# Turning the SwiGLU products of two groups at once: transposes within partition quarters and an exchange through DRAM

## The chip, the cores and the metric

The kernel runs on one core of a Trainium2 chip. The metric is device time in microseconds (us) of one execution of the whole program. Engines are named as in the profile: PE (matmul), PEld (its weight load), DVE (VectorE), ACT (ScalarE), POOL (GpSimd), SP (SyncE, whose queue issues nearly all DMAs).

## The reference

One decoder layer in float32 on x of 256 tokens by 2048 features, DEPTH 1:

```python
x = layer_norm(ALPHA * x + 0.5 * swiglu_ffn(x, ffn1_...), ln1_g, ln1_b)
u = x @ w_in + b_in                     # q, k, v and the convolution's input
mixed = concat([attention(q, k, v, sinks), conformer_conv(conv_in)]) @ w_out + b_out
x = layer_norm(ALPHA * x + mixed, ln2_g, ln2_b)
x = layer_norm(ALPHA * x + 0.5 * swiglu_ffn(x, ffn2_...), ln3_g, ln3_b)

def swiglu_ffn(x, w_gate, w_up, w_down):
    h = silu(x @ w_gate) * (x @ w_up)   # 256 x 5632
    return h @ w_down
```

The two FFNs hold most of the work: three matrices of 2048 x 5632 each. The change is in them alone.

## The kernel before, in words

Every matrix operand is split into a high and a low part of the matmul's reduced float32 type: ACT casts the raw tile to `hi` (L133) and DVE subtracts it to get `lo` (L135). A product is then three matmuls, `hi*hi`, `hi*lo` and `lo*hi` (`mm3`, L466 to L468), added up in PSUM.

**Order of the work.** Each engine runs its instructions in the order in which the program writes them; waits are semaphores. The class `Steps` sets that order by hand. A step is one weight tile of 128 x 1024: its 12 matmuls for both token blocks of 128, then `st.step()`, which runs what is due by the table `later` (`st.at(delay, work, after)`), splits up to two weight tiles ahead, and then runs what is due with `after` set. Weights come by SP into `raw` (4 buffers), are split into `hi` and `lo` (8 buffers each, RING), and may run LEAD = 7 tiles ahead of PE. A `raw` buffer is loaded anew as soon as both its readers are through, so SP's weight load waits for DVE's `lo`.

**An FFN.** The 5632 hidden features are 44 chunks of 128. They are taken in parts, `(0, JA)` and `(JA, JT)` with JA = 24, so 24 and then 20 chunks. In a part, first groups of two chunks: eight steps give gate and up products for 256 features in PSUM, with tokens on the partitions (`token_group`). `group` then applies Silu on ACT (`sl`, L658) and multiplies on DVE (`ht`, L659). The down product contracts over the features and needs them on the partitions, so `turn` (L666) transposes: DVE's transpose works in blocks of 32 x 32, and one instruction covers 32 partitions and 128 columns, reading one quarter of the partitions (t) and writing another (f). That is 16 instructions for a group, four in each of steps 1 to 4 after the group; in step 5 ACT casts the result to `hh` (L670) and DVE forms `hl` (L671). When the part's groups are done, `tokens_by` runs the down products: for each of four blocks c of 512 output columns, half as many steps as the part has chunks; at a block's end DVE adds the PSUM sum to `xt` (`evacuate`, L299). `psB` and `psC` have two PSUM buffers each, used in turn by the groups' products and the column blocks' sums.

Between the FFNs stand the mixer (attention and convolution) and the layer norms. `prepare3` loads the last layer norm's rows and has ACT load its square root table. It is called after the last group of FFN2 and before its last down products.

## Time and profile before

| | us |
|---|---|
| runs | 1716.37 median of 3 (1715.96 to 1716.41) |
| the profiled execution, span from first to last instruction | 1713.9 |
| PE busy | 1702.6 |
| PEld busy | 1416.3 |
| DVE busy, of it transposes L666 | 1183.7, 212.8 |
| ACT busy | 808.7 |
| POOL busy | 206.2 |
| down products of FFN1 begin | 266.16 (first part) |

The profiled execution's own time is its span of 1713.9 us; the runs' times are 2.5 us longer, for what lies around the span. Busy times of the engines overlap. A line of the profile that names groups reads: line of the kernel, engine, operation, output<-inputs, shapes, count, then busy time and mean ns of one, then idle time of the engine before them with what ended it. A line of a timeline gives the start, the duration and the same names. A line on DMAs gives KB each and the median time from issue to landing. A line on waits gives who waited for whom, total, times and the longest.

### The profile page before, as it was taken

To read this page: it belongs to the slowest core of one execution; us is meant where nothing else is said; L and a number is where in the kernel's file an instruction comes from. 1 tells how busy PE (TensorE), PEld (TensorE's weight loads), DVE (VectorE), ACT (ScalarE), POOL (GpSimd) and SP (SyncE) were. 2 spreads that over 40 slices of the span, in tenths; PEclk is the share of its full clock that TensorE was granted. 3 is DMA by queue.
4 is the path that set the end of the run, shared out by engine and by line. 5 is a ranking of instruction groups with operands and counts; after the bars stand their busy time and mean duration, and the time that the engine had idled before them with its cause. 6 is when DMAs were issued, how large, how long until landed. Compare 5 with 4: busy or idle time off the path is not lost.

```text
span 1713.9 us, 21604 instructions
## 1 busy us (share of the span) xinstructions
PE 1702.6 (99%) x7857; PEld 1416.3 (83%) x7857; DVE 1183.7 (69%) x2021; ACT 808.7 (47%) x1044; POOL 206.2 (12%) x116
## 2 busy tenths in 40 slices
PE   9999999999999999999999999999999999999997
PEld 7888888888888888888888888888888888888886
DVE  7877776545777765658888788877764467777655
ACT  6544444334444443477665465444443344444431
POOL 0000000000000000168996200000000000000000
PEclk9999999999999999999999999999999999999999
DMA  9766655666656656555754557655556656665662
GB/s 317 259 205 194 195 191 192 196 196 190 193 195 195 191 191 196 170 176 190 203 178 159 196 187 244 209 196 192 192 189 201 194 190 195 196 193 191 233 206 75
DMA packets 96299, 336.38 MB, mean 196 GB/s; under 512 B 11200, under 2 KB 11328, under 8 KB 95936
## 3 DMA queue, kind: packets, MB, share of 16 engines
q1 hardware_dynamic: 96048, 334.74, 60.7%
q8 instruction: 61, 1.00, 0.2%
q14 instruction: 46, 0.38, 0.1%
q10 hardware_dynamic: 144, 0.26, 0.0%
HBM read 332.86 MB, written 2.10 MB: 195 GB/s over the span
## 4 chain that ended last, share of the span: by engine, by line
PE 99%; DVE 0%; DMA 0%; ACT 0%; issue 0%; DVEq 0%; SPq 0%
PE grp L468 18%; PE grp L467 18%; PE grp L466 18%; PE acc L466 11%; PE acc L467 11%; PE acc L468 11%; PE in_c L789 2%; PE in_a L789 2%; PE in_q L789 1%; PE in_a L787 1%; PE in_c L787 1%; PE grp L487 1%; PE grp L488 1%; PE grp L485 1%; PE in_q L787 1%; PE tp L339 0%
## 5 line engine op out<-in xcount | busy, mean ns | idle before, releaser
L133 ACT CAST hi<-raw 128x1024 fp32r<-128x1024 f32 (+1 forms) x616 | 643.0, 1047 | 762.7 <-PE grp L468 357.9
L135 DVE TENSOR_TENSOR lo<-raw,hi 128x1024 fp32r<-128x1024 f32 (+1 forms) x543 | 660.4, 1221 | 386.2 <-ACT hi L133 382.1
L466 PE MATMUL grp<-hi,xcat 128*128 128x512 f32 x1384 | 538.4, 389 | 0.0
L467 PE MATMUL grp<-lo,xcat 128*128 128x512 f32 x1384 | 538.4, 389 | 0.0
L468 PE MATMUL grp<-hi,xcat 128*128 128x512 f32 x1384 | 538.4, 389 | 0.0
L467 PEld LDWEIGHTS grp<-lo,xcat 128*128 128x128 f32 x1384 | 259.8, 188 | 54.1
L466 PEld LDWEIGHTS grp<-hi,xcat 128*128 128x128 f32 x1384 | 259.8, 188 | 53.9
L468 PEld LDWEIGHTS grp<-hi,xcat 128*128 128x128 f32 x1384 | 259.8, 188 | 53.8
L466 PE MATMUL acc<-hi,hh 128*128 128x512 f32 x708 | 274.7, 388 | 0.0
L468 PE MATMUL acc<-hi,hl 128*128 128x512 f32 x708 | 274.6, 388 | 0.0
L467 PE MATMUL acc<-lo,hh 128*128 128x512 f32 x708 | 274.6, 388 | 0.0
L135 POOL TENSOR_TENSOR lo<-raw,hi 128x1024 fp32r<-128x1024 f32 x73 | 175.9, 2432 | 730.3 <-ACT hi L133 723.4
L666 DVE STREAM_TRANSPOSE hf<-ht 32x128 f32<-32x128 f32 x704 | 212.8, 302 | 11.2
L466 PEld LDWEIGHTS acc<-hi,hh 128*128 128x128 f32 x708 | 132.9, 188 | 27.3
L467 PEld LDWEIGHTS acc<-lo,hh 128*128 128x128 f32 x708 | 132.9, 188 | 27.2
L468 PEld LDWEIGHTS acc<-hi,hl 128*128 128x128 f32 x708 | 132.9, 188 | 27.2
L852 DVE SCALAR_TENSOR_TENSOR conv<-hc,cw_sb,conv 128x256 f32<-128x256 f32 x231 | 96.7, 485 | 1.1
L449 POOL TENSOR_SCALAR rs_t<-rs_y,rs_w 128x1 f32<-128x1 f32 x1 | 0.3, 342 | 717.9 <-DVE rs_y L448 717.9
L299 DVE SCALAR_TENSOR_TENSOR xt<-acc,xt 128x512 f32<-128x512 f32 x46 | 31.7, 690 | 54.7 <-PE acc L468 54.7
L658 ACT ACTIVATE sl<-grp 128x256 f32<-128x256 f32 x88 | 33.6, 384 | 56.5 <-PE grp L468 52.7
L466 PE MATMUL acc<-hi,mh 128*128 128x512 f32 x128 | 50.5, 394 | 0.0
L659 DVE TENSOR_TENSOR ht<-sl,grp 128x256 f32<-128x256 f32 x88 | 36.5, 418 | 20.3 <-ACT sl L658 20.2
(149 smaller groups left out, 947.6 us busy)
## 6 DMA issues: line engine op xcount, KB each, us to landing
raw<-in_wu SPq DMA_DIRECT2D x348, 512.0 KB, 4.3
raw<-in_wd SPq DMA_DIRECT2D x176, 512.0 KB, 4.3
raw<-in_win SPq DMA_DIRECT2D x52, 512.0 KB, 4.0
raw<-in_wout SPq DMA_DIRECT2D x32, 512.0 KB, 4.0
xt<-in_xT SPq DMA_DIRECT2D x8, 256.0 KB, 5.8
raw<-in_head SPq DMA_DIRECT2D x8, 256.0 KB, 4.7
xt<-in_x SPq DMA_DIRECT2D x2, 1024.0 KB, 8.0
rg<-in_rows SPq DMA_DIRECT2D x8, 256.0 KB, 4.4
```

The source lines that it names most:

```text
L133: nc.scalar.copy(hi, raw)
L135: eng.tensor_tensor(out=lo, in0=raw, in1=hi.bitcast(F32), op=ALU.subtract)
L299: nc.vector.scalar_tensor_tensor(out=y, in0=ps, scalar=factor, in1=x_, op0=ALU.mult, op1=ALU.add)
L466: nc.tensor.matmul(ps, s_hi, m_hi, start=start, stop=False)
L467: nc.tensor.matmul(ps, s_hi, m_lo, start=False, stop=False)
L468: nc.tensor.matmul(ps, s_lo, m_hi, start=False, stop=stop)
L658: nc.scalar.activation(sl, ps[b][:, : JG * P], AF.Silu)
L659: nc.vector.tensor_tensor(out=ht[:, b], in0=sl, in1=ps[b][:, JG * P :], op=ALU.mult)
L666: nc.vector.transpose(dst[:, t], src[:, f])
L787: nc.tensor.matmul(ps[:, :S], w[1][:, n], x1[:, k, 0, :], start=False, stop=k == KT - 1)
L789: nc.tensor.matmul(ps, w[0][:, n], x1[:, k], start=k == 0, stop=False)
L852: nc.vector.scalar_tensor_tensor(out=out, in0=x_, scalar=w, in1=acc, op0=ALU.mult, op1=ALU.add)
```

## The change

- Three parts instead of two in each FFN: 12, 16 and 16 chunks (`PARTS`).
- Two groups share one tile `ht`. After every second group one transpose of 128 x 1024 turns all 32 x 32 blocks in place, each within its own quarter of the partitions (`hr`). Four DMAs then write the quarters of `hr` to a buffer in DRAM (`far`), each in runs of 1 KB, one step later; a fifth DMA reads the buffer back as `hf` with the quarters exchanged, another step later. The cast to `hh` and the subtraction for `hl` follow two steps after that, on 1024 columns at once. `ht`, `hr` and `hf` take turns in two buffers of one tag.
- The features now lie on the partitions in another order inside four chunks; the rows of the down weights are put in the same order when the inputs are laid out (`turned`), and `block` picks the 128 x 128 block that a matmul takes.
- `down_order`: in the part of 12 chunks the first two column blocks run their first four steps each before their last two. The parts of 16 run in plain order.
- `prepare` of the last part is called 6 steps into the down products, and the rows `g3` live in another tag.

```diff
-JA = 24
+PARTS = ((0, 12), (12, 28), (28, 44))
...
+    def down_order(n):
+        half, held = n // 2, 2 if n == 12 else 0
+        order = [(c, t) for c in range(2) for t in range(half - held)]
+        order += [(c, t) for c in range(2) for t in range(half - held, half)]
+        if held == 0:
+            order.sort()
+        return order + [(c, t) for c in range(2, NC_) for t in range(half)]
...
-                def group(j, ps, hh=hh, hl=hl):
-                    ht = pool.tile([P, 2, JG * P], F32, tag="ht", name="ht")
-                    hf = pool.tile([P, JG, S], F32, tag="hf", name="hf")
+                def group(g, ps, hh=hh, hl=hl, gated=gated):
+                    if g % 2 == 0:
+                        gated[:] = [pool.tile([P, 4, 2, P], F32, tag="ht", name="ht")]
+                    f = slice(2 * (g % 2), 2 * (g % 2) + 2)
                     for b in range(2):
                         sl = pool.tile([P, JG * P], F32, tag="sl", name="sl")
                         nc.scalar.activation(sl, ps[b][:, : JG * P], AF.Silu)
-                        nc.vector.tensor_tensor(out=ht[:, b], in0=sl, in1=ps[b][:, JG * P :], op=ALU.mult)
-                    def turn(f):
+                        sides = (x_.rearrange("p (f n) -> p f n", f=2) for x_ in (sl, ps[b][:, JG * P :]))
+                        nc.vector.tensor_tensor(out=gated[0][:, f, b], in0=next(sides), in1=next(sides), op=ALU.mult)
+                    if g % 2:
+                        st.at(1, lambda ht=gated[0]: turn(g // 2, ht), True)
+
+                def turn(g, ht):
+                    hr = pool.tile([P, 4, 2 * P], F32, tag="ht", name="hr")
+                    nc.vector.transpose(hr.rearrange("p f n -> p (f n)"), ht.rearrange("p f b n -> p (f b n)"))
+                    st.vector(1.2)
+                    far = dram.tile([4, 32, 4, 2 * P], F32, tag="far", name="far")
+                    def write():
                         for t in range(4):
-                            src = ht[32 * t : 32 * t + 32].rearrange("p b (j f n) -> p f b j n", j=JG, n=32)
-                            dst = hf[32 * f : 32 * f + 32].rearrange("p j (b t n) -> p t b j n", b=2, n=32)
-                            nc.vector.transpose(dst[:, t], src[:, f])
-                    for f in range(4):
-                        st.at(1 + f, lambda f=f: turn(f), True)
-                    st.at(5, split, True)
+                            nc.sync.dma_start(far[:, :, t].rearrange("f r n -> r f n"), hr[32 * t : 32 * t + 32])
+                    def read():
+                        hf = pool.tile([P, 8 * P], F32, tag="ht", name="hf")
+                        nc.sync.dma_start(hf, far.rearrange("f r t n -> (f r) (t n)"))
+                        st.at(2, lambda: split(hf), True)
+                    def split(hf):
+                        full = hf.rearrange("p (t k i) -> p k t i", t=4, k=8)
+                        hi, lo = (x_[:, g].rearrange("p b j (t i) -> p (b j) t i", t=4) for x_ in (hh, hl))
+                        nc.scalar.copy(hi, full)
+                        nc.vector.tensor_tensor(out=lo, in0=full, in1=hi.bitcast(F32), op=ALU.subtract)
+                    st.at(1, write, True)
+                    st.at(2, read, True)
...
+    def turned(w):
+        return w.reshape(JT // 4, 4, 4, 32, D).swapaxes(1, 2).reshape(DFF, D)
```

How DVE's order moves, at the first down products of an FFN1 part with plain order. Before, from the last product `ht` of the first part to the first evacuation (`grp`: sums of a group; `acc`: sums of a column block; the weights' `lo` stand once a step):

```order
L659 TENSOR_TENSOR ht<-sl,grp_2102 128x256
L135 TENSOR_TENSOR lo_2288<-raw_2207,hi_2287 128x1024
L666 STREAM_TRANSPOSE hf<-ht 32x2x2x32 x4
L135 TENSOR_TENSOR lo_2310<-raw_2227,hi_2309 128x1024
L666 STREAM_TRANSPOSE hf<-ht 32x2x2x32 x4
L135 TENSOR_TENSOR lo_2332<-raw_2245,hi_2331 128x1024
L666 STREAM_TRANSPOSE hf<-ht 32x2x2x32 x4
L135 TENSOR_TENSOR lo_2354<-raw_2263,hi_2353 128x1024
L666 STREAM_TRANSPOSE hf<-ht 32x2x2x32 x4
L135 TENSOR_TENSOR lo_2376<-raw_2291,hi_2375 128x1024
L671 TENSOR_TENSOR hl_143<-hf,hh_142 128x512
```

With the change, at the second part (the first of 16 chunks) of FFN1:

```order
L680 TENSOR_TENSOR ht<-sl,grp_2729 128x2x128
L135 TENSOR_TENSOR lo_2895<-raw_2818,hi_2894 128x1024
L687 STREAM_TRANSPOSE hr<-ht 128x1024
L135 TENSOR_TENSOR lo_2916<-raw_2836,hi_2915 128x1024
L135 TENSOR_TENSOR lo_2938<-raw_2854,hi_2937 128x1024
L135 TENSOR_TENSOR lo_2958<-raw_2872,hi_2957 128x1024
L135 TENSOR_TENSOR lo_2976<-raw_2898,hi_2975 128x1024
L704 TENSOR_TENSOR hl_1626<-hf,hh_1625 128x1024
L135 TENSOR_TENSOR lo_2996<-raw_2919,hi_2995 128x1024
L135 TENSOR_TENSOR lo_3014<-raw_2941,hi_3013 128x1024
L308 SCALAR_TENSOR_TENSOR xt<-acc_2880,xt 128x512
```

The four small transposes of each of four steps have become one in step 1, and `hl` still stands in step 5; the first evacuation follows two steps after it now, where it came after six more before.

SP's order with the change at the same place; before, only the weight loads stood there:

```order
L93 DMA raw_2898<-in_wd 128x1024
L93 DMA raw_2919<-in_wd 128x1024
L693 DMA far<-hr 32x4x256 x4
L93 DMA raw_2941<-in_wd 128x1024
L697 DMA hf<-far 128x1024
L93 DMA raw_2961<-in_wd 128x1024
L93 DMA raw_2979<-in_wd 128x1024
```

The four writes have moved in behind the weight load of step 2, and the read behind that of step 3, where it waits for the writes to land.

## The prediction

> **What bounds the kernel now.** I read the page's first two parts first, then who TensorE (PE) waited for, then a table by stage.

> ```profile
> span 1713.9 us, 21604 instructions
> PE 1702.6 (99%) x7857; PEld 1416.3 (83%) x7857; DVE 1183.7 (69%) x2021; ACT 808.7 (47%) x1044; POOL 206.2 (12%) x116
> PEclk9999999999999999999999999999999999999999
> ...
> engine line waited for: us in total, times, longest us
> PE idle L245 <- DVE ones L242: 1.2, 1, 1.2
> PE grp L560 <- ACT hi L133: 0.2, 1, 0.2
> ```

> PE is busy for 1702.6 of 1713.9 us at full granted clock (tenths, 9 is 90% or more), and the list of its waits has two entries, 1.4 us in all, both before or at the first product of FFN1. After that it never waits for another engine. Busy PE alone does not prove that it runs at its peak, since matmuls overlap in the record, so I look at its rate in stages with different load on VectorE (DVE).

> ```profile
> core 0: us, PE busy (x) PEld busy (x) DVE busy (x) ACT busy (x) POOL busy (x), PEclk, DMA share, GB/s
> 100.00:200.00 100.00, 100.00 (x443) 82.82 (x442) 72.16 (x123) 44.45 (x51) 0.00 (x0) 1.00 0.61 193
> 300.00:400.00 100.00, 100.00 (x443) 82.84 (x442) 49.67 (x44) 38.40 (x38) 0.00 (x0) 1.00 0.61 190
> ```

> From 100 to 200 us the kernel makes gate and up products and DVE is busy for 72 us with transposes among its work; from 300 to 400 us it makes down products and DVE is busy for 50. PE issues 443 matmuls in both, one each 0.226 us. So the rate is PE's own, and work taken off DVE cannot raise it. What is left outside is the head and the tail:

> ```profile
> 4.76 0.86 PE L560 MATMUL grp<-hi,xcat 128*128 128x512 f32 x2 [0.20 <-ACT hi L133]
> ...
> 1703.74 0.28 PE L468 MATMUL acc<-hi,hl 128*128 128x256 f32 x1
> 1704.06 0.43 DVE L299 SCALAR_TENSOR_TENSOR acc<-acc,xt 128x256 f32<-128x256 f32 x1 [0.54 <-PE acc L468]
> ```

> The first product stands at 4.76, the last matmul starts at 1703.74, and some 10 us of normalising and storing follow, in which no transpose stands. The change touches neither.

> **The change part by part.** DVE first.

> ```profile
> L135 DVE TENSOR_TENSOR lo<-raw,hi 128x1024 fp32r<-128x1024 f32 x535 | 654.9, 1228 | 385.3 <-ACT hi L133 381.1
> L666 DVE STREAM_TRANSPOSE hf<-ht 32x128 f32<-32x128 f32 x704 | 212.8, 302 | 11.2
> L659 DVE TENSOR_TENSOR ht<-sl,grp 128x256 f32<-128x256 f32 x88 | 36.5, 418 | 20.3 <-ACT sl L658 20.2
> L299 DVE SCALAR_TENSOR_TENSOR xt<-acc,xt 128x512 f32<-128x512 f32 x46 | 31.7, 690 | 54.7 <-PE acc L468 54.7
> L671 DVE TENSOR_TENSOR hl<-hf,hh 128x512 fp32r<-128x512 f32 x44 | 30.2, 685 | 0.0
> ...
> L133 ACT CAST hi<-raw 128x1024 fp32r<-128x1024 f32 x608 | 638.0, 1052 | 761.4 <-PE grp L468 357.9 <-PE acc L468 299.0 <-issue 53.7
> ...
> L670 ACT CAST hh<-hf 128x512 fp32r<-128x512 f32 x44 | 27.4, 622 | 12.3 <-DVE hf L666 12.3
> ```

> Removed: 704 transposes (212.8 us) and 44 subtractions hl (30.2). Added: 22 transposes of 128x1024. The trace has none. Bounds: 1.23 us, the subtraction over the same 1024 columns, and 2.42, eight times the 302 ns of 128 columns. The 256-column product and the 1024-column subtraction (418 and 1228 ns) give 1.055 ns a column and 148 ns fixed, so 128 columns would be 283; 302 is near that, so a transpose goes at about that pace and I take 1.23: 27 us. Then 22 hl of 1024 columns (27 us) and 16 more evacuations, 8 a part in two more parts (11 us). DVE: 1183.7 - 243.0 + 65 = about 1006 us. ACT: 44 casts of 0.62 become 22 of 1.05, 4 us less. All of this lies beside PE and is worth 0 us; the evacuations would cost only if a PSUM buffer came free late, and c+2, the next user of one, starts a whole column block later (two steps later in the 12-chunk part, 5.4 us against 0.69).

> [...]

> Moved: the products now become usable only after a round trip. That is free as long as it ends before PE reads them. It is tight at one kind of place: the end of a part's gate and up products, where the last pair of groups is turned while the down products already run. Before, the last group alone was read there, after 11 or 9 steps of down products. Now the last pair is read after 8 steps in the 12-chunk parts, by their order, but after 6 in the four 16-chunk parts. I lay the new order on the old clock of the first such place:

> ```profile
> 266.16 0.39 PE L466 MATMUL acc<-hi,hh 128*128 128x512 f32 x1
> ...
> 282.48 0.39 PE L466 MATMUL acc<-hi,hh 128*128 128x512 f32 x1
> 282.70 0.39 PE L467 MATMUL acc<-lo,hh 128*128 128x512 f32 x1
> 282.93 0.39 PE L468 MATMUL acc<-hi,hl 128*128 128x512 f32 x1
> ...
> 267.77 1.23 DVE L135 TENSOR_TENSOR lo<-raw,hi 128x1024 fp32r<-128x1024 f32 x1 [0.52 <-ACT hi L133]
> 268.91 1.24 DVE L666 STREAM_TRANSPOSE hf<-ht 32x128 f32<-32x128 f32 x4
> 270.21 1.23 DVE L135 TENSOR_TENSOR lo<-raw,hi 128x1024 fp32r<-128x1024 f32 x1
> 271.46 0.33 SPq L93 DMA_DIRECT2D raw<-in_wd  x1
> ```

> The down products begin at 266.16 and a step is 12 matmuls: six steps end at 282.48, so 2.72 us each. At 282.48 PE needs hh of the last pair, at 282.93 hl. The path to it:

> - lo of step 1 ends at 267.77 + 1.23 = 269.00; the transpose, next on DVE, at 270.23; lo of step 2 at 271.46, the same moment as now, when four small transposes stand there.
> - SP then issues that step's weight load (0.33) and the four writes, queued behind it, at 0.43 each by the bias row below: the last starts at 271.79 + 3 x 0.43 = 273.1.
> - Its landing is not in the trace. Bounds:

> ```profile
> out<-xt SPq DMA_DIRECT2D x7, 256.0 KB, 2.6
> ...
> cw_sb<-in_cw SPq DMA_DIRECT2D x1, 124.0 KB, 4.1
> ...
> raw<-in_wu SPq DMA_DIRECT2D x9, 512.0 KB, 3.6
> ...
> raw<-in_wd SPq DMA_DIRECT2D x7, 512.0 KB, 4.3
> ...
> 51.57 0.43 SPq L264 DMA_DIRECT2D bias<-in_b_in  x1
> ```

>   2.6 us for stores to DRAM at the end, with no loads beside them, and 4.1 for cw_sb, 124 KB in rows of 992 bytes (the write's own size) issued just behind a weight load. So it lands at 275.7 to 277.2. The read waits for that in SP's queue, behind step 3's load.
> - The read is as large as a weight load: 3.6 us (the loads of 48 to 70 us) to 4.3 (here). It lands at 279.3 to 281.5.
> - The cast hh 1.05 and then hl 1.23: hl is ready at 281.6 to 283.8.

> Against 282.93 that is 1.3 us early to 0.9 late; the middle, 282.7, is 0.2 early. I take the middle: no stall. With the slow transpose (2.42) the late end is 2.1. Nothing makes up for a stall, so each place adds its lateness in full: 4 x (0 to 0.9) = 0 to 3.6 us, up to 8.4 with the slow transpose. In mid-part pairs the same path has a whole part's time.

> [...]

> Queued behind the waits: on SP, the weight loads. On ACT the hh cast holds up the next hi, which in turn holds up lo and a load. The read can hold SP until 277.2, the cast ACT until 282.6 instead of 280.0.

> ```profile
> SPq L93 <- DVE lo L135: 1093.1, 493, 9.3
> ...
> q1 hardware_dynamic: 96048, 334.74, 60.7%
> ```

> SP spends 1093 us waiting for a buffer to be split (total, times, longest), so it has room. A raw buffer is refilled four steps (10.9 us) before its split and lands in 4.3, which leaves 6.6 us; and the splits run up to LEAD = 7 tiles ahead, which is six steps or 16 us. Delays of 3 us vanish in that: 0 us. The 110 added DMAs move 22 x 2 x 512 KB = 23 MB, 7% on top of a queue that is busy 60.7% of the span.

> **The sum.** Removed from PE's path: 0. Added: 0, bounds 0 to 3.6. The profiled execution spans 1713.9 us and the median of the runs is 1716.4, 2.5 us outside the span; both stay: **1716.4 us**.

> **The rivals.** Faster or slower means by over 0.2% (3.4 us), about what a measurement of this kernel can tell from no change.

> - *Late exchange (slower).* The same path, at its late end. It decides from 0.86 us late at each of the four places, that is hl after 283.8. For it: the write and the read are two full landings in a row, behind loads in one queue. Against it: each row must sit at its worst end. Its price: 0.9 to 2.1 at four places, 1720.0 to 1724.8 us. [...]
> - *Starved weights (slower).* SP stands on the write's landing at each of the 22 pairs, and the loads behind it are late. It decides from 16 us of delay, against 3 by the sum above. If the write and the read each held SP for 9.3 us, the longest wait that it has now, 18.6 - 16 = 2.6 us would come through; at two pairs 5.2 us, 1721.6.
> - *Relief (faster).* The 178 us less on DVE shorten PE's interval. 443 matmuls at either DVE load speak against it; all of PE's waits are 1.4 us, so 1715.0 is the most that waits can give, still within 0.2%. To be seen, the interval would have to shrink by 0.0005 us over 7857 matmuls (4 us, 1712).

> **How the numbers follow.** Forecast (no stall, or stalls under 3.4 us in sum) 0.80; late exchange 0.13; starved weights 0.04; relief 0.03. So faster 0.03, same 0.80, slower 0.17. The range goes from 1715.4 (1.0 of the 1.4 us of waits) to 1720.8 (4 x 1.1 us late, into the first rival).

> **What would show it.** Right: PE again with 443 matmuls in each 100 us of the FFNs and no waits for hh or hl; DVE near 1006 us; a transpose near 1.23 us; hf landing at 279 to 281.5 on this clock. Wrong: rows of PE waiting for hh or hl at the four 16-chunk places, with their lateness adding up to the difference; a write landing over 4.1 us; ACT's hi waiting for weight loads more than now; or a matmul interval that differs from 0.226 us.

## The result, and the profile after

| | before | with the change |
|---|---|---|
| median of 4 runs each (lowest to highest), us | 1716.21 (1715.96 to 1716.41) | 1727.63 (1724.29 to 1728.49) |
| ratio, 95% interval | 1 | 1.0063 (1.0049 to 1.0077) |
| profiled execution: time, span, us | 1716.37, 1713.9 | 1727.47, 1725.6 |
| mean granted clock | 0.998 | 0.996 |

The kernel became 11.4 us slower. The forecast was 1716.4 us, no change. The page's first lines after, and its list of waits (engine and line, what it waited for: us in total, times, longest):

```profile
span 1725.6 us, 21097 instructions
PE 1708.5 (99%) x7857; PEld 1418.1 (82%) x7857; DVE 1006.4 (58%) x1333; ACT 802.4 (47%) x1022; POOL 206.3 (12%) x116
...
PE acc L475 <- ACT hh L703: 3.7, 2, 2.1
PE acc L477 <- DVE hl L704: 2.1, 4, 0.5
PE idle L254 <- DVE ones L251: 1.2, 1, 1.2
PE grp L575 <- ACT hi L133: 0.2, 1, 0.2
```

PE now has two entries that it did not have: it waits for hh at two places and for hl at four, 5.8 us together. That is half of the loss only. PE's timeline shows the places (start, duration, and in brackets the idle time before and what ended it); these are three of the four, at the turn from gate and up products to down products of the 16-chunk parts:

```profile
391.41 0.39 PE L477 MATMUL acc<-hi,hl 128*128 128x512 f32 x1
393.38 0.50 PE L475 MATMUL acc<-hi,hh 128*128 128x512 f32 x1 [1.58 <-ACT hh L703]
...
394.64 0.56 PE L477 MATMUL acc<-hi,hl 128*128 128x512 f32 x1 [0.52 <-DVE hl L704]
...
398.39 0.39 PE L477 MATMUL acc<-hi,hl 128*128 128x512 f32 x1
...
656.82 0.39 PE L477 MATMUL acc<-hi,hl 128*128 128x512 f32 x1
657.36 0.50 PE L475 MATMUL acc<-hi,hh 128*128 128x512 f32 x1
657.70 0.40 PE L476 MATMUL acc<-lo,hh 128*128 128x512 f32 x1
658.62 0.50 PE L477 MATMUL acc<-hi,hl 128*128 128x512 f32 x1 [0.53 <-DVE hl L704]
...
1639.82 0.39 PE L477 MATMUL acc<-hi,hl 128*128 128x512 f32 x1
1642.28 0.50 PE L475 MATMUL acc<-hi,hh 128*128 128x512 f32 x1 [2.07 <-ACT hh L703]
...
1647.76 0.39 PE L476 MATMUL acc<-lo,hh 128*128 128x512 f32 x1
```

A matmul start should follow the last by 0.226 us. From 391.41 to 398.39 there are 12 of them, worth 2.7 us, in 6.98: 4.3 lost. From 1639.82 to 1647.76 there are 14, worth 3.2, in 7.94: 4.8 lost. From 656.82 to 658.62 there are 3, in 1.80: 1.1 lost, with the slow start after it 1.2. The fourth place, at 1378, has the same form as this one and loses 1.2. Together 11.5 us, and the spans differ by 11.7. All of the loss stands at four places of a few microseconds.

Why do the first and the last lose so much more than their waits? The table by the stretches of 3.41 us that follow each other there (us and count of PE, weight loads, DVE, ACT, POOL; then the granted clock, DMA share, GB/s):

```profile
core 0: us, PE busy (x) PEld busy (x) DVE busy (x) ACT busy (x) POOL busy (x), PEclk, DMA share, GB/s
391.53:394.94 3.41, 1.30 (x5) 0.59 (x4) 1.58 (x2) 2.66 (x3) 0.00 (x0) 1.00 0.15 61
394.94:398.35 3.41, 3.41 (x9) 2.64 (x8) 1.92 (x2) 0.28 (x1) 0.00 (x0) 0.50 0.45 147
...
1640.80:1644.22 3.42, 1.41 (x5) 0.89 (x6) 1.22 (x1) 3.00 (x4) 0.00 (x0) 1.00 1.00 257
1644.22:1647.63 3.41, 3.41 (x10) 2.63 (x9) 2.36 (x2) 1.41 (x2) 0.00 (x0) 0.50 0.99 356
```

After each of the two long waits the granted clock is 0.50 for 3.41 us, with matmuls every 0.427 us. That loses 3.41 x (1 - 0.226/0.427) = 1.6 us a time, in which PE counts as busy and no list of waits shows anything.

What is late is the exchange. At the four places, from the chain of waits (start, duration, what): the last of the four writes until its landing, then the read; at the third place also the issue of the first write, 1.22 us.

```profile
382.39 3.79 DMA far<-hr
386.24 6.02 DMA hf<-far
...
647.81 4.63 DMA far<-hr
652.59 3.65 DMA hf<-far
...
1367.06 1.22 SPq L693
...
1369.32 3.81 DMA far<-hr
1373.19 3.68 DMA hf<-far
...
1631.59 3.52 DMA far<-hr
1635.28 5.89 DMA hf<-far
```

Against the prediction's own path, counted from each part's first down product (375.32, 640.73, 1361.42 and 1623.73 us; in the prediction 266.16):

| us after the first down product | predicted | 375 | 641 | 1361 | 1624 |
|---|---|---|---|---|---|
| transpose ends | 4.1 | 3.9 | 3.9 | 3.9 | 3.9 |
| last write issued | 6.9 | 7.1 | 7.1 | 7.9 | 7.9 |
| last write landed | 9.5 to 11.0 | 10.9 | 11.7 | 11.7 | 11.4 |
| read landed | 13.1 to 15.3 | 16.9 | 15.5 | 15.4 | 17.4 |
| hl ends | 15.4 to 17.6 | 19.3 | 17.8 | 17.8 | 19.8 |
| PE needs hl | 16.8 | 16.8 | 16.8 | 16.8 | 16.8 |
| late by | 0 to 0.9 | 2.5 | 1.1 | 1.0 | 3.0 |

The lateness sums to 7.6 us, the two stretches of half clock to 3.2. Of the 0.7 left most are slow starts after the waits, where one matmul follows another by 0.34 us (as from 657.36 to 657.70).

The terms that lie beside PE came as forecast. The groups of instructions after (count | busy us, mean ns of one | idle before):

```profile
L308 DVE SCALAR_TENSOR_TENSOR xt<-acc,xt 128x512 f32<-128x512 f32 x62 | 42.8, 690 | 73.8 <-PE acc L477 73.8
...
L687 DVE STREAM_TRANSPOSE hr<-ht 128x1024 f32<-128x1024 f32 x22 | 27.2, 1239 | 0.0
L704 DVE TENSOR_TENSOR hl<-hf,hh 128x1024 fp32r<-128x1024 f32 x22 | 27.0, 1226 | 83.3 <-ACT hh L703 83.3
```

And the DMA issues (count, KB each, median us from issue to landing):

```profile
far<-hr SPq DMA_DIRECT2D x88, 128.0 KB, 4.8
...
hf<-far SPq DMA_DIRECT2D x22, 512.0 KB, 3.7
```

### The profile page after: what moved, and what is told of

It reads as the page before. It is cut to its first block, busy times and chain, and to the rows that moved or that the text cites. A ratio compares the mean times of both kernels' runs of the same rounds, so it can differ in the third digit from the quotient of the medians.

```text
span 1725.6 us, 21097 instructions
## 1 busy us (share of the span) xinstructions
PE 1708.5 (99%) x7857; PEld 1418.1 (82%) x7857; DVE 1006.4 (58%) x1333; ACT 802.4 (47%) x1022; POOL 206.3 (12%) x116
## 4 chain that ended last, share of the span: by engine, by line
PE 95%; DMA 2%; DVE 1%; ACT 1%; SPq 1%; issue 0%; DVEq 0%
PE grp L476 18%; PE grp L475 18%; PE grp L477 18%; PE acc L477 10%; PE acc L475 10%; PE acc L476 10%; PE in_c L822 2%; PE in_a L822 2%; PE in_q L822 1%; DMA hf<-far 1%; DMA far<-hr 1%; PE in_a L820 1%; PE in_c L820 1%; PE grp L502 1%; PE grp L503 1%; PE grp L500 1%
## 5 line engine op out<-in xcount | busy, mean ns | idle before, releaser
L133 ACT CAST hi<-raw 128x1024 fp32r<-128x1024 f32 (+1 forms) x616 | 639.6, 1044 | 710.9 <-PE grp L477 374.6
L135 DVE TENSOR_TENSOR lo<-raw,hi 128x1024 fp32r<-128x1024 f32 (+1 forms) x543 | 658.2, 1221 | 485.7 <-ACT hi L133 481.0
L135 POOL TENSOR_TENSOR lo<-raw,hi 128x1024 fp32r<-128x1024 f32 x73 | 176.0, 2435 | 737.5 <-ACT hi L133 730.5
L476 PEld LDWEIGHTS acc<-lo,hh 128*128 128x128 f32 x708 | 133.7, 189 | 27.4
L308 DVE SCALAR_TENSOR_TENSOR xt<-acc,xt 128x512 f32<-128x512 f32 x62 | 42.8, 690 | 73.8 <-PE acc L477 73.8
L704 DVE TENSOR_TENSOR hl<-hf,hh 128x1024 fp32r<-128x1024 f32 x22 | 27.0, 1226 | 83.3 <-ACT hh L703 83.3
L703 ACT CAST hh<-hf 128x1024 fp32r<-128x1024 f32 x22 | 23.1, 1050 | 87.0 <-DMA hf<-far 87.0
## 6 DMA issues: line engine op xcount, KB each, us to landing
raw<-in_wu SPq DMA_DIRECT2D x348, 512.0 KB, 4.3
raw<-in_wd SPq DMA_DIRECT2D x176, 512.0 KB, 4.3
raw<-in_win SPq DMA_DIRECT2D x52, 512.0 KB, 4.1
raw<-in_wout SPq DMA_DIRECT2D x32, 512.0 KB, 3.7
hf<-far SPq DMA_DIRECT2D x22, 512.0 KB, 3.7
xt<-in_xT SPq DMA_DIRECT2D x8, 256.0 KB, 5.7
raw<-in_head SPq DMA_DIRECT2D x8, 256.0 KB, 4.9
```

What stands on the lines that cost most here:

```text
L133: nc.scalar.copy(hi, raw)
L135: eng.tensor_tensor(out=lo, in0=raw, in1=hi.bitcast(F32), op=ALU.subtract)
L308: nc.vector.scalar_tensor_tensor(out=y, in0=ps, scalar=factor, in1=x_, op0=ALU.mult, op1=ALU.add)
L476: nc.tensor.matmul(ps, s_hi, m_lo, start=False, stop=False)
L703: nc.scalar.copy(hi, full)
L704: nc.vector.tensor_tensor(out=lo, in0=full, in1=hi.bitcast(F32), op=ALU.subtract)
```

## The experiments

The theory after this: the whole loss is the exchange of the last pair arriving late at the four 16-chunk places, plus the clock that its longest waits cost. Rivals: that three parts instead of two cost something by themselves, that DVE's or SP's new order delays weights all along, or that the 23 MB of traffic do.

### Each half of the change apart

Two parts with the exchange kept:

```diff
-PARTS = ((0, 12), (12, 28), (28, 44))
+PARTS = ((0, 24), (24, 44))
```

> The exchange alone: the change with the two parts of 24 and 20 chunks put back. The last pair is read after 10 or 8 steps, 27.2 or 21.8 us after the down products begin; in the changed kernel hl stood 17.8 us (and 19.3 us with a slow read) after that point. Late exchange: no waits of PE, 1716 us (1715.5 to 1717.0). If the exchange costs something wherever it stands: above 1719 us.

Measured 1716.15 us (1715.53 to 1716.48), ratio 1.000 (0.9991 to 1.0009), and no wait of PE behind the head. DVE is busy for 995.8 us. The 22 exchanges and their traffic cost nothing where the down products leave them more steps. The new place of `prepare` is in this kernel too, so it costs nothing by itself either.

Three parts with the small transposes kept in place of the exchange (shown against the change; `prepare` stays where it was before):

```diff
-                hr = pool.tile([P, 4, 2 * P], F32, tag="ht", name="hr")
-                nc.vector.transpose(hr..., ht...)
+                        ht = pool.tile([P, 2, JG * P], F32, tag="ht", name="ht")
+                        hf = pool.tile([P, JG, S], F32, tag="hf", name="hf")
...
+                    for f in range(4):
+                        st.at(1 + f, lambda f=f: turn(f), True)
```

> The parts alone: the kernel before with three parts of 12, 16 and 16 chunks in the new order, and the old transposes on the chip. hl of the last group stands at 280.15 - 266.16 = 14.0 us after the down products begin, and is now read after 7 steps (19.0 us). Late exchange: no waits of PE, 1716 us (1715.5 to 1717.0). If more part ends or 16 more evacuations cost by themselves: above 1719 us.

Measured 1716.36 us (1716.08 to 1716.88), ratio 1.0003 (0.9993 to 1.0013), DVE busy for 1193.7 us, no wait of PE. Neither half costs anything alone. It is the meeting of the exchange's length with the six steps that the 16-chunk parts leave it.

### The same exchange, read later

The change holds back the last two tiles of the 12-chunk parts until the steps before them are done; the same for the 16-chunk parts:

```diff
-        half, held = n // 2, 2 if n == 12 else 0
+        half, held = n // 2, 2
```

> The change with one thing moved: in the parts of 16 chunks, too, the first two column blocks leave their last two steps for later, so the last pair is read after 12 steps of down products, 32.6 us after they begin, and not after 6. Late exchange as the whole cause: PE waits for no hh and no hl, the granted clock stays at 1.0 through the FFNs, and the time is back at 1716 us (1715.5 to 1717.0). Starved weights, or any cost of the added DMAs apart from these four places: PE waits remain for hi or lo, and the time stays above 1719 us.

Measured 1716.12 us, ratio 1.0001 (0.9992 to 1.001). This edit also moves the second half of the mixer's output projection, which uses the same order; there products and weights no longer belong together, so this kernel does not compute the layer, though it runs as many instructions as the next one, 21101. Therefore the edit was limited to the FFN:

```diff
-        half, held = n // 2, 2 if n == 12 else 0
+        half, held = n // 2, 2 if n in (12, 16) else 0
```

> The changed kernel with the last two steps of the first two column blocks put off in the parts of 16 chunks as in those of 12, and nothing else: the order of the output projection stays as it was. The last pair is read after 12 steps, 32.6 us after the down products begin. Late exchange as the whole cause: no waits of PE for hh or hl, clock 1.0 through the FFNs, 1716 us (1715.5 to 1717.0). Any other cost of the change: above 1719 us.

Measured 1716.31 us (1715.54 to 1716.68), ratio 1.000 (0.999 to 1.0009). The page and the waits of this kernel:

```profile
span 1714.7 us, 21101 instructions
...
PE idle L254 <- DVE ones L251: 1.2, 1, 1.2
PE grp L575 <- ACT hi L133: 0.2, 1, 0.2
```

Same three parts, same transposes, same traffic, with medians of 4.8 us for a write and 3.7 for a read as with the change. At the four places hl still ends 17.7 to 18.2 us after the first down product, past the 16.8 of the changed kernel's order. Only the moment at which PE reads the last pair differs, and the whole 11.4 us is gone, the half clock with it. That settles that the lateness at the four places is the cause. It also shows what the change is worth when nothing is late: 0, with 179 us less on DVE.

### Which part of the exchange is late

Four kernels move the issues. First both the writes and the read ahead of the weight load of their step in SP's queue:

```diff
-                    st.at(1, write, True)
-                    st.at(2, read, True)
+                    st.at(1, write)
+                    st.at(2, read)
```

> The change with the four writes and the read each put ahead of the weight load of their step in SP's queue, and so ahead of the wait for that step's lo. The writes can start when the transpose ends, some 1.7 us earlier (379.25 against 380.96 at the second part's end). Late exchange, with the place in the queue as the part that was too long: hl comes 1.2 to 1.7 us earlier; the two places that were 1.1 us late (1.2 us lost each) become free; those with a slow read stay 1 to 1.6 us late and keep the clock; 1716.5 to 1720 us. If the landing is set by the DMA engines' other traffic and not by the place in the queue: as the changed kernel, 1724 to 1729 us.

Measured 1716.13 us (1715.88 to 1717.30), ratio 1.0002 (0.9992 to 1.0011), just under the 1716.5 to 1720 expected. Its DMA issues and its wait for hl:

```profile
far<-hr SPq DMA_DIRECT2D x88, 128.0 KB, 3.5
...
hf<-far SPq DMA_DIRECT2D x22, 512.0 KB, 5.6
```

```profile
PE acc L477 <- DVE hl L704: 0.5, 1, 0.5
```

The writes start at the transpose's end and land in 3.5 instead of 4.8 us, but the reads take 5.6 instead of 3.7: a gain on one side, a part of it given back on the other. What remains is one wait of 0.5 us, at the last place. Two of the four places still have a slow read (5.79 and 6.08 us), and these had been expected to keep the half clock; none does, because the last write lands 1.7 to 3.3 us earlier than with the change. Only the writes ahead:

```diff
-                    st.at(1, write, True)
+                    st.at(1, write)
```

> The change with the four writes alone put ahead of their step's weight load; the read stays behind step 3's. The writes land some 8.4 to 9.4 us after the down products begin instead of 10.9 to 11.7, and the read follows within 1.5 us of step 3's load. If the distance to the last load decides how long a read takes, nearly all take over 5 us and eat the gain in part: hl at 16.5 to 17.7 us against the 16.8 at which PE needs it, 1716.5 to 1720 us. If it does not: reads of 3.3 to 4 us, hl at 14.5 to 15.5 us, no waits, 1716 us.

Measured 1717.85 us (1716.27 to 1719.34), ratio 1.0009 (0.9999 to 1.0018). Only the read ahead:

```diff
-                    st.at(2, read, True)
+                    st.at(2, read)
```

> The change with the read alone put ahead of its step's weight load, right behind the four writes. It still waits for them to land, some 11 us after the down products begin, but the last load before it is now step 2's, issued some 6 us earlier, and none is in flight. In the runs so far reads took 3.2 to 4.2 us where the last load had been issued over 3.1 us before, and 5.2 to 6.5 where under 3.0. If that distance decides: all reads outside the stretch with the residual rows near 1045 us take under 4.3 us, hl stands 17.1 us after the down products begin, 0.3 to 0.5 late, PE's waits stay short, the clock at 1.0, 1717 to 1720 us. If slow reads come by chance or from the write just before: about 6 of 22 stay over 5 us, and where one falls on a part's end the clock drops: 1720 to 1727 us.

Measured 1718.29 us (1716.82 to 1719.53), ratio 1.0012 (1.0002 to 1.0021). The reads and the waits of the two, the writes-ahead kernel first (its profiled execution was the slowest of its ten, 1719.34 us):

```profile
hf<-far SPq DMA_DIRECT2D x22, 512.0 KB, 5.5
...
PE acc L477 <- DVE hl L704: 1.5, 4, 0.5
```

```profile
hf<-far SPq DMA_DIRECT2D x22, 512.0 KB, 3.4
...
PE acc L477 <- DVE hl L704: 0.9, 2, 0.5
```

With only the read ahead all 22 reads land in 3.11 to 4.33 us; with only the writes ahead 20 of 22 take over 5. Each alone brings back over 9 of the 11.4 us, the one by the writes, the other by the reads. What differs in the reads is how long before the read SP issued its last weight load: right behind the writes the read waits for their landing, and no load stands close before it; with the writes ahead, step 3's load goes out 0.5 to 2 us before the read. In the changed kernel the same split is seen. There 16 of 22 reads take 3.3 to 4.0 us, with the last load at least 2.8 us before, mostly over 3.2; five take 5.6 to 6.4, with it 2.7 to 3.2 us before (one more takes 7.0, in a stretch with other loads). The two long places are two of the five. So the 6.02 us read at 386.24 goes with a pattern: a read that follows a 512 KB load by less than about 3 us mostly takes some 2 us more.

The traces show a sharper form of it. In the changed kernel the 16 quick reads were issued when the load before them had 1.05 to 1.30 us left until its landing, the five slow ones when it had 1.72 to 1.95. Over the eight kernels with the exchange, and apart from the stretch near 1040 us, 1.6 us left divides reads of under 4.6 us from longer ones with 5 exceptions in 168; a distance of 3.0 us from the load's issue has 14. So what goes with a slow read is a load still well short of landing. This dividing line was fitted to the runs afterwards; why it is a step of 2 us and not a gradual delay, no run here shows. `prepare`'s row loads, which stand beside the read of the last place, do not by themselves explain that read: they stand there in the kernel with the late reader too, whose read takes 4.04 us.

Is it the place in SP's queue, or the traffic? The writes issued from ACT:

```diff
-                            nc.sync.dma_start(far[:, :, t]..., hr[32 * t : 32 * t + 32])
+                            nc.scalar.dma_start(far[:, :, t]..., hr[32 * t : 32 * t + 32])
```

> The change with the four writes issued from ACT's queue instead of SP's; the read stays on SP. On ACT they stand behind the hi of step 2, which ends some 0.1 us before the transpose does, so they start some 1.6 us earlier than on SP behind the wait for lo and the weight load. Late exchange, set by the place in the issuing queue: as with the writes and the read ahead on SP, 1716 to 1720 us. If it is the DMA engines' shared traffic that makes the landing late: 1724 to 1729 us. A cost of its own: four issues on ACT (some 0.43 us each) ahead of the next hi, 1.7 us at each of 22 pairs, hidden by the splits' lead.

Measured 1724.16 us (1722.03 to 1728.64), ratio 1.0051 (1.0033 to 1.0068). Its DMA issues and its waits:

```profile
far<-hr ACTq DMA_DIRECT2D x88, 128.0 KB, 5.0
...
hf<-far SPq DMA_DIRECT2D x22, 512.0 KB, 5.6
```

```profile
PE acc L475 <- ACT hh L703: 3.6, 3, 1.5
PE acc L477 <- DVE hl L704: 1.6, 3, 0.5
```

The writes start 1.7 us earlier, at the transpose's end, yet land no sooner after their issue (5.0). At the four places the last one lands 0.2 to 1.2 us earlier than with the change. But the reads take 5.6 us in the median: at these places SP has issued step 3's load only 2.0 to 2.4 us before them. So 7.8 of the 11.4 us stay. A queue of its own did not make a write quicker here (5.0 against 4.8 us); what holds it up, no run separates. Standing ahead of the load in the same queue (3.5 and 3.9 us) is worth more.

### What a wait costs beside itself

The half clock after two of the waits was measured on the kernel before, where nothing else is late. The split of the last group is put off to the step before PE reads it, and idle subtractions on DVE make hl late by a chosen amount at its four part ends:

```diff
+                        for _ in range(extra if j == n - JG else 0):
+                            nc.vector.tensor_tensor(out=ht..., in0=hf..., in1=hf..., op=ALU.subtract)
                         nc.vector.tensor_tensor(out=hl[:, js], in0=hf, in1=hh[:, js].bitcast(F32), op=ALU.subtract)
...
-                    st.at(5, split, True)
+                    st.at(n // 2 - 1 if j == n - JG else 5, split, True)
```

With 0, 2, 3 and 1 of them:

> The price of one PE wait, in the kernel before: at each of the four part ends the last group's cast and subtraction are put off to the step just before PE reads them (11 or 9 instead of 5), and 0, 2, 3 and 1 idle subtractions of 128x512 (0.685 us each) stand on DVE ahead of hl, so that hl is late by about 0.4, 1.8, 2.5 and 1.1 us in the order of the program. If a wait costs its length alone: 5.8 us in sum, 1722 us, clock 1.0 at all four. If a PE idle for some 2 us of a 3.4 us window loses half its clock for the next 3.4 us, as the changed kernel's two long places suggest: the same 5.8 us and 1.7 us more at the wait of 2.5, perhaps at 1.8: 1724 to 1726 us. [...]

Measured 1722.37 us (one run, as for the two kernels after it). The places lose 0, 1.3, 2.1 and 0.6 us beside the clock, each 0.4 to 0.5 less than set, so the time alone would fit the first case. The clock speaks against it: it halves after the third wait, and after that alone. With 4, 6, 5 and 8:

> The same with 4, 6, 5 and 8 idle subtractions: hl late by about 3.1, 4.5, 3.8 and 5.9 us, 17.3 us in sum. Waits alone: 1733.5 us, clock 1.0. Half clock for 3.4 us after a wait of over 2 us: a drop at all four, 1.7 us each, 1740 us. [...]

Measured 1736.42 us, between the 1733.5 of waits alone and the 1740 with four drops. The clock halves after the second and the fourth, where the matmuls stand 4.46 and 5.90 us apart. It does not after the first (3.00 us apart), nor after the third, which is longer (3.73 us apart, a wait of 3.34) than some that did it. Before both drops a whole stretch held no busy PE. The earlier drops came without that: the stretches before them held 1.52 us of busy PE in the kernel above, and 1.30 and 1.41 in the changed one. The third place in the timeline, and the stretches around it:

```profile
1289.49 0.50 PE L468 MATMUL acc<-hi,hl 128*128 128x512 f32 x1 [3.34 <-DVE hl L674]
```

```profile
1284.62:1288.03 3.41, 1.53 (x7) 0.94 (x5) 3.31 (x5) 1.05 (x1) 0.00 (x0) 1.00 0.58 210
1288.03:1291.45 3.42, 1.96 (x9) 1.62 (x10) 2.06 (x4) 0.00 (x0) 0.00 (x0) 1.00 0.05 19
```

So the length of the wait does not decide. Four equal ones then, 4 subtractions each:

> The kernel before with four idle subtractions ahead of the last hl at all four part ends: four waits of PE of one length, about 2.8 us, 11 us in sum. If the granted clock is set over windows of 3.41 us that run freely from the start, and a window with over some 2 us of idle PE halves the next one, then one length gives both outcomes: a drop where the window holds over 2 us of the wait, none where the wait is cut by a window's edge into pieces under 2 us. Time 1728 us with no drop, 1.7 us more for each. If the length alone decides: all four alike.

Measured 1730.78 us. All four waits are 2.61 us, and the clock halves after one of them only. The stretches of 3.41 us, laid out through the whole run from the drop at 1285.21, at the first place, the third and the fourth:

```profile
295.35:298.76 3.41, 1.47 (x7) 0.89 (x5) 3.31 (x6) 1.05 (x1) 0.00 (x0) 1.00 0.63 216
298.76:302.18 3.42, 2.75 (x12) 2.29 (x13) 1.45 (x4) 0.14 (x1) 0.00 (x0) 1.00 0.03 13
...
1281.80:1285.21 3.41, 1.41 (x7) 0.83 (x5) 3.31 (x6) 1.05 (x1) 0.00 (x0) 1.00 0.61 202
1285.21:1288.63 3.42, 2.81 (x7) 2.25 (x8) 1.25 (x2) 0.00 (x0) 0.00 (x0) 0.50 0.05 19
1288.63:1292.04 3.41, 3.41 (x10) 2.67 (x9) 1.54 (x2) 1.04 (x1) 0.00 (x0) 0.50 0.00 0
...
1629.95:1633.37 3.42, 1.77 (x8) 1.13 (x6) 3.32 (x5) 1.26 (x2) 0.00 (x0) 1.00 0.88 315
```

Where a stretch held 1.41 us of busy PE the next one ran at half clock; with 1.47 or 1.77 it did not. The half clock lasted two stretches here, 6.8 us, as it did after the fourth wait of the kernel before. That such stretches follow each other through a run is seen in the changed kernel: its two drops begin at 394.94 and 1644.22 us and end at 398.35 and 1647.63, and the 1249.28 us between their beginnings are 366 times 3.413 us. On the grid laid out so, the four equal waits differ in how an edge divides them, and the wait of 3.34 us above, cut by the edge at 1288.03 with 1.53 and 1.96 us of busy PE on its two sides, cost nothing beside itself.

How much busy PE in a stretch goes with full clock in the next is not settled. Over these three kernels, the changed one and the one with the writes on ACT, stretches at full clock with 1.30 to 1.41 us of it, or none, always halved the next, and those with 1.94 or more never did. Between these both came about: 1.47, 1.53, 1.77 and 1.86 did not, while 1.52 did, and so did 1.86 in the kernel with the writes on ACT, after waits of 1.03 and 0.53 us:

```profile
1377.60:1381.02 3.42, 1.86 (x8) 0.93 (x7) 1.43 (x2) 2.51 (x3) 0.00 (x0) 1.00 0.44 180
```

The recorded ends of matmuls are modelled, so the busy times are rough. Whether that accounts for the overlap, or something else counts too, stays open.

## Why the prediction was wrong

- **What bounds the kernel** was right. PE's rate away from the four places is unchanged, and every kernel here whose transposed products are in time takes 1716 us, with DVE busy for 996 or for 1194 us. Relief (1712 us) is out.
- **The costs beside PE** were right: DVE was forecast at about 1006 us (1006.4), the transpose of 128x1024 at 1.23 us (1.239), ACT at 4 us less (6.3 less).
- **Starved weights** are out: two parts with the same 22 exchanges cost nothing.
- **The moved path** was laid out on the right places and in the right order, and its first two terms held at 375 and 641 us. At 1361 and 1624 us the last write went out 0.9 us later than forecast, since the first of the four took 1.2 us to issue (the row of 1.22) and not 0.43.
- **The step that failed is the two landings and the choice of their middle.** The write was bounded by 2.6 to 4.1 us; the last one took 3.5 to 4.6 at the places (all 88 have a median of 4.8). The read was bounded by 3.6 to 4.3 and took 3.65, 3.68, 5.89 and 6.02. None of the rows behind the bounds was a write with loads beside it: they were stores at the end, one load of 124 KB behind a weight load, weight loads at the head and seven in one stretch of the middle. The upper end, taken as the worst, was too low for the usual write, and no bound at all for a read behind a load still well short of landing, for which the sum has no term. Where "the middle, no stall" stood there was a stall at all four places, of 1.0 to 3.0 us, past the late end of 0.9 each time.
- **A term was missing**: PE's clock after a wait, 3.2 us of the 11.4. A wait was priced at its length alone.
- **The rival "late exchange"** was the mechanism, with a chance of 0.13. Its price, 1720.0 to 1724.8 us, stopped at 2.1 us late a place; 2.5 and 3.0 were reached, and the clock came on top. What stood against it there, "each row must sit at its worst end", took the bounds from less loaded transfers as if both ends were equally likely in a queue that is busy 60.7% of the span.

## What to carry to other kernels

A path that ends within its own uncertainty of a deadline, on an engine without slack, is not "no stall": price it at the landings of loaded queues (here 4.8 us for a write in the median and 5.6 to 6.4 for a slow read, where 4.1 and 4.3 had been taken as the worst), and count the slower ones as the rule. Two cheap remedies each brought the whole loss back: the reader moved back, from 6 steps after the part's end to 12, and the small transfers and their read issued ahead of the large loads in the same queue. And some 2 us of waiting on PE within a stretch of 3.41 us cost 1.6 us more than itself for each stretch at half clock (1.30 and 1.41 us of busy PE, at 391.53 and 1640.80 in the changed kernel), though not every time (1.47 us, no drop), in time that the profile counts as busy: look at the granted clock right behind it.
